# Two products of four column groups at the head of an MLP's up-projection

## The chip, the cores and the metric

One core of a Trainium2 chip runs the kernel. The metric is device microseconds of one execution, taken as the median of a few runs. The profile is of one more execution, with an instruction trace; its clock readings start at the first instruction.

## The reference

One layer of a hybrid decoder on x of 2048 positions by 1024 columns, float32. A mixer comes first (windowed attention beside a short convolution, with projections in and out), then

```python
x = x + y @ w_out[l]
hm = rms_norm(x, mlp_norm_g[l])
x = x + jnp.square(jax.nn.relu(hm @ w_up[l])) @ w_down[l]
```

with `w_up` 1024 x 4096 and `w_down` 4096 x 1024. The change is in the product `hm @ w_up`.

## The kernel before, in words

Every product of two float32 matrices is made of three passes of TensorE: an operand is split into a high part (a cast on ScalarE) and the rest (a subtraction on DVE), and high x high, high x low and low x high are summed in PSUM.

The up-projection works by Strassen's scheme in Winograd's form: seven products of blocks in place of eight, with sums of blocks before and behind them. The positions are two blocks of 1024 (`tb` 0 and 1), each 2 x 2 blocks of 512 x 512; the 4096 columns of `w_up` are 16 groups (`NCG`) of 256. A group n counts through both blocks, so n is 0 to 31, and a step of the loop is one product (n, p), p from 1 to 7: `NB` = 4 slices of 128 rows by three passes, 12 matmuls of 128x512 (L1118 to L1127). Products 1 and 2 add up in one PSUM bank, so do 5 and 3, and 7 and 4; banks tagged "at" (4) serve 1, 2, 5 and 3, those tagged "mm" (3) the others (L1115 to L1117).

The x operands of a block are seven matrices of 1 MiB, one a product p, that were written to DRAM (`xop_dram`) and are loaded in two halves of 512 KiB by `load_op` (L800), cast (L806) and subtracted (L807). They stay in the 14 `op` buffers for all 16 groups. The operands of block 0 are written by the last part of the mixer; those of block 1 are made during block 0 by the generator `prepare_rest` (L931), which takes one of its pauses at every step: it reads rows of `x1_dram` (L940), norms them (L943 to L946), transposes (L959), subtracts on GpSimd and stores (L977). What is left of it when the operands of block 1 are asked for is run at once (L1041).

The weights of a group are four pieces of 256 KiB (`Weights.pieces`, L838: for p = 1, 2, 7, 4), loaded at L849 in rows of 512 bytes. `sums` (L854) makes two more pieces on DVE (for 5 and 6) and changes that of 7 on GpSimd; `last` (L864) makes that of 3 on GpSimd. There are 18 buffers "w" for pieces. `split_up` (L869) casts and subtracts one product's piece (L872, L873).

`up_out` (L876) empties the PSUM bank behind a product: product 1 is copied to `u2` (L896), 2 gives a first result `f11` (relu and square on ScalarE, L899 and L888), which goes to DRAM (L882), 6, 5, 7, 3 and 4 add to it on DVE (L885), and behind 3 and 4 GpSimd forms four sums and differences (L814) that go to DRAM as well. Each kind of these tiles has one to three buffers (`UP_BUFS`, L60), and "st" has five, used by `prepare_rest`.

The order of the steps is the list `seq` (L992 to L1009). Each pass of the loop asks for the x operands of the step five ahead (`ready_x`, L1113) and for the weights of the step three ahead (`ready`, L1114), and then issues the 12 matmuls. Loads of x, of weights and of rows are all issued on the SP queue; a scheduler of the language may issue an instruction ahead of one that the code names first when its engine is free. The writes of the last chunk's rows to `x1_dram` come from GpSimd's queue (L634).

Of the kernel before, what the change touches and what calls it, by code (L numbers as in the profile page):

```python
# [52 lines left out]
NCG = DFF // (2 * P)  # L53
NTB = S // (2 * BW)

FIRST = (1, 6, 2)
LEAD, LEAD_DOWN = 3, 2
NOP = 14
DOWN_BUFS = {"u": 4, "x1": 5}
# [26 lines left out]
def hymba_layer(  # L86
# [44 lines left out]
    def bank(tag, name):  # L131
        return psum.tile([P, 512], F32, tag=tag, name=name, bufs=BANKS[tag])
# [29 lines left out]
    def rsqrt(dst, ms):  # L162

        nc.gpsimd.tensor_scalar(ms, ms, EPS, None, op0=ALU.add)
        nc.gpsimd.tensor_tensor(dst, ms, mhalf[:, : ms.shape[1]], op=ALU.pow)
# [647 lines left out]
    def tt(dst, a, b, op=ALU.subtract):  # L813
        nc.gpsimd.tensor_tensor(dst, a, b, op=op)  # L814


    def piece(tag, name):
        return pool.tile([P, BW], F32, tag=tag, name=name, bufs=UP_BUFS[tag])

    def pieces(blk):  # L820
        return blk.rearrange("p (k c) -> p k c", k=NB)
# [54 lines left out]
    def up_out(n, p, ps, v):  # L876

        tb, n = divmod(n, NCG)
        nm = f"{tb}_{n}"

        def put(i, b, eng):
            eng.dma_start(fop_dram[tb][ORDER_DOWN.index(i)][n // 2][:, n % 2], b)  # L882

        def add(dst, b):
            nc.vector.tensor_tensor(dst, ps, b, op=ALU.add)  # L885

        def square(b):
            nc.scalar.activation(b, b, AF.Square)  # L888

        def relu2(b):  # L890
            nc.scalar.activation(b, b, AF.Relu)  # L891
            square(b)

        if p == 1:
            v["u2"] = piece("u2", f"u2_{nm}")
            nc.scalar.copy(v["u2"], ps)  # L896
        elif p == 2:
            v["11"] = piece("f11", f"f11_{nm}")
            nc.scalar.activation(v["11"], ps, AF.Relu)  # L899
            square(v["11"])  # L900
            put(1, v["11"], nc.scalar)
        elif p == 6:
            add(v["u2"], v["u2"])
        elif p == 5:
            v["u4"] = piece("u4", f"u4_{nm}")
            add(v["u4"], v["u2"])
        elif p == 7:
            add(v["u4"], v["u4"])
            relu2(v["u4"])
            put(4, v["u4"], nc.scalar)  # L910
        elif p == 3:
            v["12"] = piece("f12", f"f12_{nm}")
            add(v["12"], v["u2"])
            relu2(v["12"])
            s1 = piece("s1", f"s1_{nm}")
            tt(s1, v["12"], v["u4"], ALU.add)
            put(5, s1, nc.gpsimd)
            v["s2"] = piece("s2", f"s2_{nm}")
            tt(v["s2"], s1, v["11"])
            put(6, v["s2"], nc.gpsimd)  # L920
            tt(v["12"], v["11"], v["12"])
            put(7, v["12"], nc.gpsimd)
        else:
            add(v["u2"], v["u2"])
            relu2(v["u2"])
            put(2, v["u2"], nc.scalar)
            s4 = piece("s4", f"s4_{nm}")
            tt(s4, v["u2"], v["s2"])
            put(3, s4, nc.gpsimd)

    def prepare_rest():  # L931

        xs = {}

        def fetch(t):
            for i in range(2):
                nm = f"m{2 + i}_{t}"
                r = 2 * BW + i * BW + t * P
                xt = pool.tile([P, D], F32, tag="xt", name=f"xt_{nm}", bufs=2)
                nc.sync.dma_start(xt, x1_dram[r : r + P, :])  # L940
                junk = piece("st", f"junk_{nm}").bitcast(BF16)[:, :D]
                ss = small.tile([P, 1], F32, tag="ss", name=f"ss_{nm}", bufs=2)
                nc.scalar.activation(junk, xt, AF.Square, scale=D**-0.5, accum_out=ss)  # L943
                rs = small.tile([P, 1], F32, tag="rs", name=f"rs_{nm}", bufs=2)
                rsqrt(rs, ss)
                nc.vector.tensor_scalar(xt, xt, rs, None, op0=ALU.mult)  # L946
                xs[i] = xt

        fetch(0)
        for _ in range(7):  # L950
            yield
        for t in range(NT):
            b = {}
            for i in range(2):
                for k in range(2):
                    nm = f"m{2 + i}_{t}_{k}"
                    pt = bank("tr", f"pt_{nm}")
                    for j in range(NB):
                        nc.tensor.transpose(  # L959
                            pt[:, j * P : (j + 1) * P], xs[i][:, (NB * k + j) * P : (NB * k + j + 1) * P], ident  # L960
                        )
                    b[k, i] = piece("st", f"st_{nm}")
                    nc.vector.tensor_tensor(
                        pieces(b[k, i]),
                        pieces(pt),
                        g_cols[:, NB * k : NB * (k + 1), None].to_broadcast([P, NB, P]),
                        op=ALU.mult,
                    )
                    yield
                    yield  # L970
            if t + 1 < NT:
                fetch(t + 1)
            yield

            def put(i, blk, t=t):
                dst = xop_dram[1][ORDER.index(i)].rearrange("p (k c) -> p k c", k=NB)
                nc.sync.dma_start(dst[:, :, t * P : (t + 1) * P], pieces(blk))  # L977

            b11, b21, b12, b22 = b[0, 0], b[1, 0], b[0, 1], b[1, 1]
            put(1, b11)  # L980
            put(2, b21)
            put(3, b22)
            for _ in range(3):
                yield
            for i, dst, b0, b1 in ((5, b11, b12, b11), (7, b12, b22, b12), (6, b22, b22, b11), (4, b21, b21, b22)):
                tt(dst, b0, b1)
                put(i, dst)
                yield

    seq, nf = [], 0  # L992

    def firsts(n):

        nonlocal nf
        for n in range(nf, min(n + 1, NTB * NCG)):
            yield from ((n, p) for p in FIRST)
        nf = max(nf, n + 1)

    for n in range(NTB * NCG):
        if not n:
            seq += sorted(firsts(1), key=lambda x: (1, 2, 6).index(x[1]))
        elif n % NCG in (0, NCG - 2):
            seq += firsts(n + 1)
        between = iter(list(firsts(n + 1)))
        for p in (5, 7, 3, 4):
            seq.append((n, p))
            seq += [x for x in (next(between, None),) if x]  # L1009
# [1 line left out]
    for i, (n, p) in enumerate(seq):  # L1011
        uses.setdefault((n // NCG, p), []).append(i)
    wts, wops, xops, ps, vs = {}, {}, {}, {}, {}
    others = prepare_rest()

    def ready(i):

        if i >= len(seq):
            return
        n, p = seq[i]  # L1020
        if n < 2 and p < 3:
            wts[n].piece(p, 1, p)
        if p == 1 and n > 1 or p == 6 and n == 1:
            for m in range(n, n + (3 if n > 1 else 2)):
                if m < NTB * NCG and m not in wts:
                    wts[m] = Weights(m)
        if p == 6 or p == 1 and n > 1:
            for m in range(n, n + (2 if p == 1 else 1)):
                if m < NTB * NCG and 5 not in wts[m].w:
                    wts[m].sums()  # L1030
        if p == 3:
            wts[n].last()
        wops[i] = split_up(wts[n].w[p], f"{n}_{p}")
# [64 lines left out]
    fill = ops.tile([P, 24], F32, tag="fill", name="fill")  # L1098
    nc.gpsimd.memset(fill, 0.0)

    for n in range(2):
        wts[n] = Weights(n, later=False)
    for i in range(LEAD):
        ready_x(i)
        ready(i)
    for i in range(LEAD, LEAD + 2):
        ready_x(i)
    for i, (n, p) in enumerate(seq):
        tb = n // NCG
        if i == len(seq) - NB:  # L1110
            for j in range(LEAD_DOWN):
                ready_down(j)
        ready_x(i + LEAD + 2)  # L1113
        ready(i + LEAD)  # L1114
        if p not in GOES_ON:  # L1115
            ps[n, AFTER.get(p)] = bank("at" if p in (1, 5) else "mm", f"u{n}_{p}")
        pt = ps[n, p if p in GOES_ON else AFTER.get(p)]  # L1117
        for k in range(NB):  # L1118
            for j, (a, b) in enumerate(((0, 0), (0, 1), (1, 0))):
                nc.tensor.matmul(  # L1120
                    pt,
                    wops[i][:, a, k, :],
                    xops[tb, p][k // 2][:, b, k % 2, :],
                    start=p not in GOES_ON and k + j == 0,
                    stop=k + j == NB + 1,
                    skip_group_check=True,
                )  # L1127
        up_out(n, p, pt, vs.setdefault(n, {}))

        if n > 1:  # L1130
            next(others, None)
    up_ctx.close()
    pool_tags.add("raw")
# [116 lines left out]
```

## Time and profile before

| what | value |
|---|---|
| runs | 2025.42, 2028.33, 2021.88 us; median 2025.42 |
| profiled execution | 2028.57 us |
| its span, first to last instruction | 2026.8 us |
| TensorE busy | 1958.5 us, 97% |
| DVE, ScalarE, GpSimd busy | 1309.6, 919.2, 607.2 us |
| mean granted TensorE clock | 0.983 |
| up-projection (L1120) | 752.2 to about 1401.6 us |

The profiled execution lasts 1.8 us longer than its span, and is 3.15 us above the median of the runs. An engine's busy time counts no DMA issue. Idle time of an engine is put down to the engine or transfer whose signal came last.

### The profile page before, as it was taken

To read this page: it belongs to the slowest core of one execution; us is meant where nothing else is said; L and a number is where in the kernel's file an instruction comes from. 1 tells how busy PE (TensorE), PEld (TensorE's weight loads), DVE (VectorE), ACT (ScalarE), POOL (GpSimd) and SP (SyncE) were. 2 spreads that over 40 slices of the span, in tenths; PEclk is the share of its full clock that TensorE was granted. 3 is DMA by queue.
4 is the path that set the end of the run, shared out by engine and by line. 5 is a ranking of instruction groups with operands and counts; after the bars stand their busy time and mean duration, and the time that the engine had idled before them with its cause. 6 is when DMAs were issued, how large, how long until landed. Compare 5 with 4: busy or idle time off the path is not lost.

```text
span 2026.8 us, 25559 instructions
## 1 busy us (share of the span) xinstructions
PE 1958.5 (97%) x9356; PEld 1632.9 (81%) x9356; DVE 1309.6 (65%) x1772; ACT 919.2 (45%) x1718; POOL 607.2 (30%) x647
## 2 busy tenths in 40 slices
PE   8999999999999987999998999999999999999989
PEld 7879887987988766888886888888788888888877
DVE  4787778678688878777868666665633434545551
ACT  5555455445555645555456455454432232231230
POOL 2231223313122324676654545544000000007000
PEclk9989999999999898999999999999999999999999
DMA  7214523352442477566757444435974447865551
GB/s 240 84 62 107 183 65 101 86 166 70 128 167 84 118 241 254 188 213 197 240 166 250 146 155 156 146 114 197 401 240 142 145 147 243 300 204 186 199 183 45
DMA packets 234190, 342.56 MB, mean 169 GB/s; under 512 B 17232, under 2 KB 148304, under 8 KB 234064
## 3 DMA queue, kind: packets, MB, share of 16 engines
q1 hardware_dynamic: 207120, 271.70, 41.9%
q0 software_dynamic: 13120, 44.05, 6.1%
q10 hardware_dynamic: 13824, 25.17, 3.3%
q8 instruction: 74, 1.21, 0.3%
q14 instruction: 52, 0.43, 0.1%
HBM read 242.31 MB, written 98.57 MB: 168 GB/s over the span
## 4 chain that ended last, share of the span: by engine, by line
PE 81%; DVE 6%; DMA 4%; POOL 3%; ACT 3%; issue 3%; SPq 0%; DVEq 0%; ACTq 0%; POOLq 0%
PE d L1212 29%; PE u L1120 26%; PE pout L212 2%; PE pout L214 2%; PE pout L213 2%; PE pz L213 2%; PE pz L212 2%; PE pz L214 2%; DMA op_x<-xop 2%; PE px_c L212 1%; PE px_c L213 1%; PE px_c L214 1%; PE pc_c L213 1%; PE pc_c L214 1%; PE pc_c L212 1%
## 5 line engine op out<-in xcount | busy, mean ns | idle before, releaser
L1120 PE MATMUL u<-op_x,wop 128*128 128x512 f32 x2688 | 624.7, 393 | 23.2 <-ACT u L896 10.0
L1212 PE MATMUL d<-op_w,op_f 128*128 128x512 f32 x2688 | 612.5, 390 | 8.5 <-DVE d L1166 6.9
L1120 PEld LDWEIGHTS u<-op_x,wop 128*128 128x128 f32 x2688 | 506.5, 189 | 134.9 <-ACT u L896 11.6
L1212 PEld LDWEIGHTS d<-op_w,op_f 128*128 128x128 f32 x2688 | 506.0, 188 | 114.8 <-issue 7.3
L807 DVE TENSOR_TENSOR op_f<-op_f 128x1024 fp32r<-128x1024 f32 x112 | 144.3, 1292 | 251.5 <-ACT op_f L806 251.4
L806 ACT CAST op_f<-op_f 128x1024 fp32r<-128x1024 f32 x112 | 117.5, 1051 | 329.3 <-DMA op_f<-fop 323.4
L873 DVE TENSOR_TENSOR wop<-wu,wop 128x512 fp32r<-128x512 f32 x160 | 190.1, 1192 | 68.2 <-ACT wop L872 68.1
L872 ACT CAST wop<-wu 128x512 fp32r<-128x512 f32 x160 | 98.7, 619 | 103.9 <-PE u L1120 92.5
L885 DVE TENSOR_TENSOR u<-u,u 128x512 f32<-128x512 f32 x128 | 87.5, 684 | 56.7 <-PE u L1120 56.4
L1075 POOL DMA_DIRECT2D wds<-raw x16 | 8.5, 534 | 333.4 <-DVE raw L1073 333.4
L807 DVE TENSOR_TENSOR op_w<-raw,op_w 128x1024 fp32r<-128x1024 f32 x56 | 73.1, 1305 | 34.0 <-ACT op_w L806 34.0
L806 ACT CAST op_w<-raw 128x1024 fp32r<-128x1024 f32 x56 | 58.9, 1052 | 64.8 <-PE d L1212 37.5
L814 POOL TENSOR_TENSOR wu<-wu,wu 128x512 f32<-128x512 f32 x32 | 42.9, 1342 | 136.6 <-DVE wu_s L859 136.6
L213 PE MATMUL pz<-w_qkv,h_h 128*128 128x256 f32 x288 | 82.3, 286 | 0.0
L212 PE MATMUL pz<-w_qkv,h_h 128*128 128x256 f32 x288 | 82.1, 285 | 0.0
L214 PE MATMUL pz<-w_qkv,h_h 128*128 128x256 f32 x288 | 81.6, 284 | 0.0
L477 POOL TENSOR_SCALAR_AFFINE_SELECT pp_b<-pp_b 128x512 fp32r<-128x512 f32 x60 | 48.3, 817 | 78.8 <-PE po_b L506 38.4
L891 ACT ACTIVATE u<-u 128x512 f32<-128x512 f32 x64 | 40.4, 632 | 65.6 <-DVE u L885 63.1
L873 DVE TENSOR_TENSOR wop<-wu_s,wop 128x512 fp32r<-128x512 f32 x64 | 65.9, 1029 | 3.1 <-ACT wop L872 3.1
L568 POOL COPY halo<-u_c 128x2 f32<-128x2 f32 x16 | 6.2, 386 | 200.2 <-DVE u_c L567 188.9
L872 ACT CAST wop<-wu_s 128x512 fp32r<-128x512 f32 x64 | 39.8, 622 | 57.4 <-PE u L1120 44.9
L814 POOL TENSOR_TENSOR s<-f,u 128x512 f32<-128x512 f32 x32 | 46.5, 1453 | 60.7 <-ACT f L888 60.7
(225 smaller groups left out, 3649.0 us busy)
## 6 DMA issues: line engine op xcount, KB each, us to landing
op_f<-fop SPq DMA_DIRECT2D x112, 512.0 KB, 4.2
raw<-in_w_down_dram SPq DMA_DIRECT2D x72, 512.0 KB, 4.2
wu<-in_w_up_dram SPq DMA_DIRECT2D x128, 256.0 KB, 3.5
fop<-s POOLq DMA_DIRECT2D x96, 256.0 KB, 2.5
fop<-u ACTq DMA_DIRECT2D x64, 256.0 KB, 3.1
op_x<-xop SPq DMA_DIRECT2D x28, 512.0 KB, 7.4
raw_qkv<-in_w_in_dram SPq DMA_DIRECT2D x11, 1024.0 KB, 5.4
x<-in_x_dram SPq DMA_DIRECT2D x20, 512.0 KB, 6.9
```

The costliest lines, as they stand in the source:

```text
L212: nc.tensor.matmul(ps, st(0), mv(0), start=first, stop=False)
L213: nc.tensor.matmul(ps, st(0), mv(1), start=False, stop=False)
L214: nc.tensor.matmul(ps, st(1), mv(0), start=False, stop=last)
L477: nc.gpsimd.affine_select(part, full, pattern=[[0, GQ], [1, P]], compare_op=ALU.is_ge, fill=0.0, base=0, channel_multiplier=-1,)
L806: nc.scalar.copy(op[:, 0], raw)
L807: nc.vector.tensor_tensor(op[:, 1], raw, op[:, 0].bitcast(F32), op=ALU.subtract)
L814: nc.gpsimd.tensor_tensor(dst, a, b, op=op)
L872: nc.scalar.copy(hi, blk)
L873: nc.vector.tensor_tensor(lo, blk, hi.bitcast(F32), op=ALU.subtract)
L885: nc.vector.tensor_tensor(dst, ps, b, op=ALU.add)
L1120: nc.tensor.matmul(pt, wops[i][:, a, k, :], xops[tb, p][k // 2][:, b, k % 2, :], start=p not in GOES_ON and k + j == 0, stop=k + j == NB + ...
L1212: nc.tensor.matmul(ps[tb][j], fs[tb][:, a, k, j * P : (j + 1) * P], w[:, b, k, :], start=first and p not in GOES_ON and k + n == 0, stop=l ...
```

## The change

The list of steps opens with products 1 and 2 of four groups (`START`) where it opened with products 1, 2 and 6 of two. Product 6 of groups 1 to 3 follows among the products 5, 7, 3, 4 of the group before. From group 4 on the list is as it was. For the first four groups a product's own piece is loaded alone (p = 1, 2); the other two pieces of groups 0 and 1 are loaded at (2,2) and (3,2), and those of 2 and 3 at (0,6) and (1,6). `prepare_rest` takes its first step at (3,5) and not at (2,1). `u2` of group 3 and `f11` of groups 2 and 3 lie in "st" buffers.

```diff
+START = 4
...
-            v["u2"] = piece("u2", f"u2_{nm}")
+            v["u2"] = piece("st" if tb == 0 and n == START - 1 else "u2", f"u2_{nm}")
...
-            v["11"] = piece("f11", f"f11_{nm}")
+            v["11"] = piece("st" if tb == 0 and START - 2 <= n < START else "f11", f"f11_{nm}")
...
-    seq, nf = [], 0
+    seq, nf = [], START
...
     for n in range(NTB * NCG):
         if not n:
-            seq += sorted(firsts(1), key=lambda x: (1, 2, 6).index(x[1]))
-        elif n % NCG in (0, NCG - 2):
+            seq += [(m, p) for p in (1, 2) for m in range(START)] + [(0, 6)]
+        elif n >= START and n % NCG in (0, NCG - 2):
             seq += firsts(n + 1)
-        between = iter(list(firsts(n + 1)))
+        between = iter([(n + 1, 6)] if n + 1 < START else list(firsts(n + 1)))
...
-    others = prepare_rest()
+    others, begin = prepare_rest(), seq.index((START - 1, 5))
...
-        if n < 2 and p < 3:
-            wts[n].piece(p, 1, p)
-        if p == 1 and n > 1 or p == 6 and n == 1:
-            for m in range(n, n + (3 if n > 1 else 2)):
+        if n < START:
+            if p < 3:
+                wts[n].piece(p, 1, p)
+
+            if p == 2 and n >= START - 2:
+                wts[n + 2 - START].pieces()
+            if p == 6:
+                wts[n].sums()
+                if n + 2 < START:
+                    wts[n + 2].pieces()
+                else:
+                    wts[n + 2] = Weights(n + 2)
+        elif p == 1:
+            for m in range(n, n + 3):
                 if m < NTB * NCG and m not in wts:
                     wts[m] = Weights(m)
-        if p == 6 or p == 1 and n > 1:
-            for m in range(n, n + (2 if p == 1 else 1)):
+            for m in range(n, n + 2):
                 if m < NTB * NCG and 5 not in wts[m].w:
                     wts[m].sums()
...
-    for n in range(2):
+    for n in range(START):
         wts[n] = Weights(n, later=False)
...
-        if n > 1:
+        if i >= begin:
             next(others, None)
```

## Rows read from the trace of the kernel before

**Rows 1.** The page, granted TensorE clock in 40 slices of 50.67 us, in tenths

```profile
PEclk9989999999999898999999999999999999999999
```

**Rows 2.** Four stretches: length, busy us of each engine (instructions), clock, DMA share, GB/s

```profile
752.00:762.00 10.00, 6.62 (x25) 4.64 (x26) 6.41 (x7) 4.10 (x7) 0.99 (x8) 1.00 1.04 407
762.00:772.00 10.00, 6.26 (x25) 4.25 (x24) 7.77 (x8) 9.14 (x13) 1.62 (x1) 1.00 1.07 373
772.00:782.00 10.00, 5.09 (x12) 3.17 (x11) 7.15 (x7) 1.89 (x3) 3.36 (x3) 0.60 1.07 346
782.00:792.00 10.00, 9.65 (x31) 7.48 (x32) 9.67 (x12) 5.95 (x9) 2.47 (x2) 0.72 0.87 243
```

**Rows 3.** TensorE's waits, 752 to 792: total us, times, longest us

```profile
PE u L1120 <- ACT wop L872: 7.0, 3, 3.0
PE u L1120 <- DVE wop L873: 3.5, 2, 2.5
```

**Rows 4.** ScalarE in order of time: start, us, line, names [idle before <-what ended it]

```profile
757.41 1.05 ACT L806 CAST op_x<-op_x 128x1024 fp32r<-128x1024 f32 x1 [1.64 <-DMA op_x<-xop]
760.52 0.62 ACT L872 CAST wop<-wu 128x512 fp32r<-128x512 f32 x1 [2.06 <-DMA wu<-in_w_up_dram]
```

**Rows 5.** DMA issues, 736 to 800 us: count, KB each, median us to landing

```profile
op_x<-xop SPq DMA_DIRECT2D x14, 512.0 KB, 8.8
...
xop<-xm SPq DMA_DIRECT2D x5, 256.0 KB, 3.1
xt_m<-x_dram SPq DMA_DIRECT2D x2, 512.0 KB, 4.5
```

**Rows 6.** TensorE in order of time, first and last of 34 matmuls

```profile
743.11 0.40 PE L214 MATMUL pout<-w_wo,at_b 128*128 128x512 f32 x1
...
750.61 0.39 PE L214 MATMUL pout<-w_wo,at_b 128*128 128x512 f32 x1
```

**Rows 7.** TensorE in order of time, 751 to 800

```profile
752.17 0.50 PE L1120 MATMUL u<-op_x,wop 128*128 128x512 f32 x1 [1.17 <-ACT wop L872]
...
754.71 5.07 PE L1120 MATMUL u<-op_x,wop 128*128 128x512 f32 x21 [1.01 <-DVE wop L873]
...
771.72 0.73 PE L1120 MATMUL u<-op_x,wop 128*128 128x512 f32 x2 [3.03 <-ACT wop L872]
774.96 4.63 PE L1120 MATMUL u<-op_x,wop 128*128 128x512 f32 x10 [2.50 <-DVE wop L873]
782.35 17.81 PE L1120 MATMUL u<-op_x,wop 128*128 128x512 f32 x66 [2.76 <-ACT wop L872]
```

**Rows 8.** ScalarE in order of time, the copy behind product (2,1)

```profile
804.28 0.59 ACT L896 COPY u<-u 128x512 f32<-128x512 f32 x1
```

**Rows 9.** DVE in order of time, GpSimd idle beside it

```profile
758.50 1.23 DVE L807 TENSOR_TENSOR op_x<-op_x 128x1024 fp32r<-128x1024 f32 x1 [1.46 <-ACT op_x L806]
761.17 0.69 DVE L873 TENSOR_TENSOR wop<-wu,wop 128x512 fp32r<-128x512 f32 x1 [1.45 <-ACT wop L872]
```

**Rows 10.** Issues of the SP queue in order of time, 742 to 790

```profile
760.52 3.77 SPq L805 DMA_DIRECT2D op_x<-xop  x3
765.28 8.57 SPq L849 DMA_DIRECT2D wu<-in_w_up_dram  x6
...
776.63 11.65 SPq L849 DMA_DIRECT2D wu<-in_w_up_dram  x8
788.33 0.97 SPq L940 DMA_DIRECT2D xt_m<-x_dram  x2
```

**Rows 11.** Groups of instructions, 788 to 860: busy us, mean ns | idle before

```profile
L873 DVE TENSOR_TENSOR wop<-wu,wop 128x512 fp32r<-128x512 f32 x18 | 23.3, 1300 | 3.8 <-ACT wop L872 3.7
...
L885 DVE TENSOR_TENSOR u<-u,u 128x512 f32<-128x512 f32 x15 | 10.2, 682 | 4.8 <-PE u L1120 4.8
...
L814 POOL TENSOR_TENSOR s<-s,f 128x512 f32<-128x512 f32 x3 | 3.9, 1304 | 0.1
```

**Rows 12.** TensorE's waits, 1040 to 1120: total us, times, longest us

```profile
PE u L1120 <- ACT u L896: 7.6, 1, 7.6
```

## The prediction, made before the changed kernel ran

> **What bounds the kernel now.** I read the busy shares by slice first. TensorE is the engine that sets the time, and its granted clock is near full but in three slices; the one inside the MLP begins at 760 us [rows 1]. So I cut the first 40 us of the MLP into four stretches: TensorE is busy for only 27.6 of 40 us, the clock falls to 0.60 and 0.72, and the DMA engines are full (share 1.04 to 1.07) until 782 us, with DVE next behind at 31.00 of 40 [rows 2]. The list of TensorE's waits there names casts and subtractions of weight pieces first [rows 3]; those engines waited for transfers in their turn, as ScalarE's own rows show: the cast of a half of x at 757.41 and that of a weight piece at 760.52 each start when a transfer lands [rows 4]. An x load took 8.8 us from issue to landing [rows 5]. So the start of the MLP is bound by transfers: 7 MiB of x operands and the weights go through one full queue, and TensorE's order asks for a new 1 MiB operand after every two products, or after one.
>
> How much is lost there: matmuls of 512 columns follow each other by 7.50 us / 33 = 0.227 us at the full clock [rows 6], so a product of 12 matmuls takes 2.73 us, and twelve products 32.7 us. In the trace the first begins at 752.17 [rows 7] and the twelfth in the order, (2,1), ends at about 804.2, when ScalarE copies it out [rows 8]: 52.0 us. The loss is 19.3 us, of which 12.4 are idle (40 less the four busy times [rows 2]). A clock of 0.60 and 0.72 over 20 us is 13.6 us at the lower of the two levels, 1.2 of 2.4 GHz [rows 2]; it starts behind the two gaps before 771.72 and 774.96 [rows 7], TensorE works in some 10 of them at half its rate, and so loses about 5. The rest are the ends of products. From 782.35 on TensorE runs without a gap that matters [rows 7]. Nothing over this 19.3 can be won.
>
> **The order of products.** Twelve products open the MLP now as (0,1) (1,1) (0,2) (1,2) (0,6) (1,6) (0,5) (0,7) (0,3) (0,4) (1,5) (2,1); after, as (0..3,1) (0..3,2) (0,6) (0,5) (1,6) (0,7). The number of matmuls is the same. Two operands now carry eight products, 21.8 us of work, in which the other five MiB can land. I follow the queue step by step.
> Until 760.52 the queue has delivered x1, x2 and three weight pieces [rows 4]. The new order has the same bytes ahead of that moment, only with the third piece before x2, so x2's second half lands at about 760.5 and not 757.4. Products (0,1), (1,1), (2,1) need x1 and one piece each: TensorE goes on where the first two now stop (754.71 + 5.07 = 759.8, of which 0.2 are the last one's end [rows 7]) and reaches 762.3. Product (3,1) has its piece behind x2: ScalarE casts x2's half (1.05) and the piece (0.62) [rows 4], DVE subtracts for the half (1.22) and the piece (0.68) [rows 9], so it is whole at 760.5 + 1.05 + 1.22 + 0.68 = 763.5. Two matmuls need no subtraction, so about 0.8 us are idle, and the product ends at 765.8.
> From 760.5 the queue moves 360 GB/s (mean of 373 and 346 [rows 2]). In the order of the new code, in MB after that point: three pieces 0.79, x6 1.84, a piece and two for group 0 2.62, x5 3.67, the piece of (3,2) 3.93, four pieces 4.98, x7 6.03, x3 7.08, two pieces 7.60, x4 8.65, and three results of 0.26 MB written meanwhile, 9.4 in all. The piece of (3,2) lands at 771.4 and is split by 773.3; TensorE wants it at 765.8 + 3 x 2.73 = 774.0. (0,6) is wanted at 776.7, with its pieces there since 767.8. (0,5) is wanted at 779.5; its cast stands behind those of x7, which lands at 777.3, so it is split at 777.3 + 1.05 + 1.22 + 0.68 = 780.2: 0.3 idle. (1,6) stands behind x3 in the same way (780.2, split at 783.1) and is wanted at 782.5: 0.3. (0,7) stands behind x4 (786.6, split at 789.6) and is wanted at 785.5: 3.6 idle if the engines keep the program's order, none if the splits are issued ahead. The twelfth product ends at about 791.8, against 804.2: **12.4 us won**; 15 to 16 with the splits ahead of x4. The engines do not always keep the order: the issue queue now has three x halves ahead of the six pieces of groups 1 and 2, and by the code it would be two [rows 10]. I take the strict order.
>
> **Weight loads.** Each product's own piece is loaded alone, and the other two of a group follow at products 2 and 6; by the time x4 is in, 16 pieces have gone and not 20. That is 1.05 MB less in the full queue, 2.9 us, and is in the sum above. The pieces of groups 4 to 6 are loaded together at (4,1), 12 of them with the first needed 3 steps or 8.2 us later; now 8 come at (2,1) into the full queue, and TensorE doesn't stop behind them [rows 7, 10]. Nothing.
>
> **The second block's preparation** starts at step 24 of the order instead of 11. Its DMA reads of rows at 788.33 [rows 10], its norms on ScalarE, GpSimd and DVE, its transposes and its seven stores per tile move later, none is added; the SP queue has weight loads alone ahead of them then. It has 71 pauses, one a step: it ends at step 95, before the change at 85. The operands are first asked for at step 104. Nine steps, 24.6 us, are left as cover; without it the cost is that of the slow case below.
>
> **Buffers.** Three results of groups 2 and 3 use the five "st" buffers, free until step 24, and are gone by step 30; no instruction is added. Four open accumulators take all four "at" banks; (0,5) wants the first one again at step 9, four steps or 11 us after (0,2) ended. Nothing.
>
> **Groups 0 to 2 closer together.** Their products 5, 7, 3, 4 and a 6 come five steps apart, 13.65 us, and not six or seven. Per group DVE has five splits and two sums (7 x 0.68) and five additions from PSUM (0.68 [rows 11]), 8.2 us; GpSimd six subtractions or additions of 1.3 [rows 11], 7.8. Each fits in 13.65, so I take 0. The other end: now, with GpSimd at work, a split takes 1.30 and not 0.68 [rows 9, 11], while the addition that reads PSUM stays at 0.68. If nothing on the two engines overlaps, a group needs 16.0 us, 2.35 too many, for three groups 7.0. The Trainium skill's "SBUF — State Buffer" (section "SBUF: two separate sides") says that DVE instructions with two SBUF inputs and GpSimd instructions lock a shared pair of ports, one blocking the other whole. The trace agrees, and by that rule the closer groups speak against the change; the lock alone would take 7 x 0.68 + 7.8 = 12.6 us of 13.65, no stop.
>
> **The sum.** The profiled execution is 2028.57 (span 2026.8 and 1.8 around it): 2028.57 - 12.4 = 2016.2. The median of the runs is 3.15 below it, so **2013.0** is the forecast. 0.3% (6.1 us) is about what a measurement of this kernel tells from no change.
>
> **Rivals.**
> A, as forecast, with 9 to 18 us won: 2007 to 2016. For it: idle time, full queue and order of use stand together in one stretch.
> B, DVE and GpSimd become the bound: at 31.00 of 40 us now [rows 2], DVE has no room for work that comes sooner, and the three groups give back 7.0: 12.4 - 7.0 = 5.4 won, 2020.0. Against it: between 788 and 860 the same mix ran beside a TensorE that never waited.
> C, the half clock stays, because the idle time of (3,1) or before (0,7) still brings it: a stretch like the present one costs about 5 us again: 7.4 won, 2018.
> D, nothing comes of it: the instruction order that is built is not the program's, as [rows 10] shows for one load, so x2 or the fourth piece waits in the queue and TensorE's idle time only moves to (3,1) and (0,7). Two to five won, about 2022.
> E, slower: at the border of the two blocks TensorE already waits 7.6 us once, behind a copy in ScalarE's queue [rows 12]. If the preparation, ten steps later than now, is not done by step 104, what is left of it runs ahead of the x loads. A tile that is left takes its read (4.5 [rows 5]), four subtractions on GpSimd (5.2 [rows 11]) and a store (3.1 [rows 5]), 12.8 us, and the load behind it 8.8; five steps (13.65) hide a part. One tile costs 8 us, two 20.8: 2025.4 - 12.4 + 20.8 = 2034. It decides when 9 of the 71 steps slip, and makes the kernel slower from some 25; by the count none does.
>
> **Chances.** A 0.57, B 0.13, C 0.12, D 0.12, E 0.06. A and C are faster by over 0.3%, and half of B: 0.75. The other half of B and D lie within: 0.19. Slower: 0.06. The range runs from all 19.3 won (2006) to the far side of D (2022); it leaves out E, and some of D.
>
> **What will show it.** Right: TensorE's idle time between 752 and 792 falls from 12.4 to under 6 us, with no clock below 0.9 there; (3,1) starts within 1.5 us of (2,1)'s end; the twelfth product ends near 792; DVE is at 35 us or more of those 40; the DMA share stays full until about 787. Wrong: a half clock after 760, a stop between 795 and 835 whose releaser is DVE or GpSimd (B), or a wait near 1069 that was 1.0 and is 10 or more (E).

## The result, and the profile after

The changed kernel takes 2012.9 us (median of 6 runs, 2010.07 to 2014.92), the one before 2024.12 beside it (6 runs). The ratio is 0.9944, with a 95% interval from 0.9931 to 0.9957: 11.3 us won, 8.7 to 14.0. The forecast was 2013.0.

The profiled execution lasts 2014.13 us, its span 2012.1. It is 14.4 us under that of before, which is more than the change gave: the mixer, whose instructions are the same and in the same order on every engine, ended 3.6 us sooner (747.4 against 751.0 us). The last section comes back to that. Times in the up-projection are therefore compared from the mixer's end; the stretches below are those of [rows 2] by the clock, and so lie 3.6 us later behind the mixer than before.

Four stretches after, for [rows 2], and the one behind them (length; busy us of PE, PEld, DVE, ACT, POOL with instructions; clock; DMA share; GB/s):

```profile
752.00:762.00 10.00, 10.00 (x46) 8.27 (x45) 6.15 (x7) 7.17 (x10) 0.33 (x5) 1.00 1.09 362
762.00:772.00 10.00, 9.34 (x42) 7.41 (x41) 7.20 (x8) 6.56 (x12) 2.63 (x2) 1.00 1.10 354
772.00:782.00 10.00, 6.78 (x27) 5.21 (x26) 9.85 (x9) 7.98 (x13) 5.80 (x4) 0.93 1.00 313
782.00:792.00 10.00, 9.72 (x39) 7.62 (x38) 10.00 (x14) 6.48 (x11) 6.64 (x6) 0.90 0.71 247
792.00:802.00 10.00, 10.00 (x46) 8.29 (x45) 10.00 (x9) 5.50 (x10) 7.91 (x8) 1.00 0.46 146
```

The DMA engines are as busy as before until 782 us, though they move 362, 354 and 313 GB/s in place of 407, 373 and 346. TensorE is busy for 35.8 of the 40 us up to 792 and not 27.6. DVE is busy for 29.85 of the 30 us from 772 on, so that it is now the next thing that can hold TensorE up. TensorE in order of time, for [rows 7]:

```profile
749.38 0.74 PE L1131 MATMUL u<-op_x,wop 128*128 128x512 f32 x2 [1.27 <-DVE op_x L809]
751.12 19.11 PE L1131 MATMUL u<-op_x,wop 128*128 128x512 f32 x83 [1.00 <-DVE wop L875]
770.89 5.75 PE L1131 MATMUL u<-op_x,wop 128*128 128x512 f32 x24 [0.66 <-DVE wop L875]
779.85 10.07 PE L1131 MATMUL u<-op_x,wop 128*128 128x512 f32 x36 [3.22 <-DVE wop L875]
```

One long run of seven products, a short wait before the third matmul of (3,2), then one wait of 3.2 us before the third matmul of (0,5), and behind it a stretch of lower clock of 3.4 us in place of 13.6. The twelfth product ends at 789.47, 42.07 us after the mixer; before it was 804.24 - 751.00 = 53.24. So 11.2 us are won there. By the 25th product, where the order is that of before again, 8.6 of them are left. TensorE's waits of 752 to 792, for [rows 3], are one row:

```profile
PE u L1131 <- DVE wop L875: 4.2, 3, 3.2
```

### The profile page after: what moved, and what is told of

Same layout as the page of the kernel before. It is cut to its first block, busy times and chain, and to the rows that moved or that the text cites. A ratio compares the mean times of both kernels' runs of the same rounds, so it can differ in the third digit from the quotient of the medians.

```text
span 2012.1 us, 25577 instructions
## 1 busy us (share of the span) xinstructions
PE 1950.2 (97%) x9356; PEld 1628.0 (81%) x9356; DVE 1312.1 (65%) x1772; ACT 919.5 (46%) x1718; POOL 611.3 (30%) x647
## 5 line engine op out<-in xcount | busy, mean ns | idle before, releaser
L875 DVE TENSOR_TENSOR wop<-wu_s,wop 128x512 fp32r<-128x512 f32 x64 | 60.3, 943 | 3.9 <-ACT wop L874 3.9
L449 ACT ACTIVATE sc_b<-sc_b,ngm_b 128x128 f32<-128x128 f32 x128 | 49.6, 390 | 28.5 <-DVE ngm_b L446 28.4
```

Of the source, the lines that this page charges most:

```text
L449: nc.scalar.activation(sc[:, hd, :], sc[:, hd, :], AF.Exp, bias=ngm[:, hd : hd + 1], accum_out=den[:, hd : hd + 1])
L875: nc.vector.tensor_tensor(lo, blk, hi.bitcast(F32), op=ALU.subtract)
```

## The experiments

Each ran five rounds beside the kernel before. "Won" is the ratio times 2024 us. One execution is profiled; "up stage" is measured in that trace, from the end of the mixer's last matmul to the end of the last up-product, so that it holds none of the mixer's spread. It has a spread of its own: "preparation late" and "group 2's pieces later", whose times can't be told from those of the kernel before, are 2.7 and 2.8 us shorter than it in this column, most of it at the border of the two blocks, where TensorE waits 7.6 us in the trace of before [rows 12] and 5.2 and 5.3 in theirs. The changed kernel waits 5.4 there, so some 2 of its 9.3 us can't be put down to the change.

| kernel | ratio, 95% interval | won, us | up stage, us |
|---|---|---|---|
| before | 1 | 0 | 650.9 |
| changed | 0.9944 (0.9931 to 0.9957) | 11.3 | 641.6 |
| START = 2 | 0.9955 (0.9938 to 0.9973) | 9.1 | 643.9 |
| START = 3 | 0.9965 (0.9951 to 0.9980) | 7.1 | 646.7 |
| whole groups loaded | 0.9969 (0.9956 to 0.9982) | 6.3 | 646.7 |
| before, preparation late | 0.9999 (0.9986 to 1.0012) | 0.2 | 648.2 |
| before, (1,6) later | 0.9985 (0.9970 to 1.0000) | 3.0 | 648.5 |
| before, group 2's pieces later | 0.9993 (0.9983 to 1.0003) | 1.4 | 648.1 |
| changed, x asked for last | 0.9966 (0.9953 to 0.9979) | 6.9 | 643.9 |
| changed, subtractions on DVE | 0.9949 (0.9936 to 0.9961) | 10.3 | 641.8 |
| before, new load plan | 0.9981 (0.9969 to 0.9994) | 3.8 | 644.9 |
| START = 2, x four ahead | 0.9988 (0.9977 to 1.0000) | 2.4 | 647.6 |
| changed, two groups on DVE | 0.9960 (0.9944 to 0.9976) | 8.1 | 641.0 |
| the same, border changed | 0.9934 (0.9919 to 0.9950) | 13.4 | 637.6 |

**Two groups in place of four.**

```diff
-START = 4
+START = 2
```

> The changed kernel with START = 2: products 1 and 2 of two groups open the MLP, (0,6) follows and (1,6) comes one place later; pieces are still loaded alone and the second block's preparation starts at (1,5). Theory O (the order: eight products on two x operands, 21.8 us of TensorE work, cover the loads of the other five): four products cover 10.9 us, 10.9 fewer than with four groups, of which the loads need nearly all, so the kernel stands near the one before, 2019 to 2025 us, with 9 us or more idle on TensorE between the first product and the twelfth. Rival W (loading pieces alone, 16 and not 20 in the full queue, is what wins): all of the weight change is here, so 2011 to 2016 us.

Theory O's total falls here: 9.1 us won, where it gave up to 5 and rival W 8 to 13. Its sign for the first twelve products holds, though: in the trace the twelfth ends 47.9 us after the mixer, 5.3 sooner than before and 5.9 later than with four groups, with 9.8 us idle behind the first matmul (O: 9 or more). The rest of the 9.1 isn't found in this trace, which is of the slowest of the seven runs (2016.94 us, median 2012.83). The stop is elsewhere than expected. TensorE's products in order of time:

```profile
758.97 3.02 PE L1131 MATMUL u<-op_x,wop 128*128 128x512 f32 x12 [1.91 <-ACT u L898]
766.77 1.22 PE L1131 MATMUL u<-op_x,wop 128*128 128x512 f32 x2 [4.79 <-ACT wop L874]
769.46 30.79 PE L1131 MATMUL u<-op_x,wop 128*128 128x512 f32 x124 [1.46 <-DVE wop L875]
```

and ScalarE's instructions ahead of that wait:

```profile
760.83 1.05 ACT L808 CAST op_x<-op_x 128x1024 fp32r<-128x1024 f32 x1 [1.92 <-DMA op_x<-xop]
...
762.26 1.05 ACT L808 CAST op_x<-op_x 128x1024 fp32r<-128x1024 f32 x1
...
763.70 1.04 ACT L808 CAST op_x<-op_x 128x1024 fp32r<-128x1024 f32 x1
...
765.17 1.04 ACT L808 CAST op_x<-op_x 128x1024 fp32r<-128x1024 f32 x1
...
766.10 0.62 ACT L874 CAST wop<-wu 128x512 fp32r<-128x512 f32 x1
```

The wait of 4.8 and 1.5 us stands before (1,2), whose piece had landed at 758.7; its cast stands behind those of four halves of x6 and x5 that were still coming in. After it 124 matmuls run without a stop. So with two groups the queue of ScalarE is what is waited for, once, and the later waits of the kernel before, 3.0 and 2.5 us at (0,6) and 2.8 before (1,6) [rows 7], are gone.

**Three groups** (`START = 3`).

> The changed kernel with START = 3: six products on x1 and x2, 16.4 us. Theory O: between, 2014 to 2020 us, some 5 us more idle than with four groups in the first twelve products. Rival W: as the changed kernel, 2011 to 2015 us. If DVE and not the transfers is what the wait before (0,5) hangs on, three groups may lose little: 2013 to 2016 us with a wait of 4 to 6 us before the first product on x5.

2015.7 us and 7.1 won lie in O's range, but fewer than with two groups (the intervals overlap). The profiled execution shows how little that says: TensorE's idle time in the first 100 us is 8.5 us (changed kernel 9.0, START = 2 10.6, before 13.4), yet the lower clock was granted for 17.1 us there and cost 8.0, against 1.7 in the changed kernel; 6.8 of the 17.1 us began 2.6 us after the mixer's end, in the first product, which stands in the same place in both. In idle time three groups do as well as four.

**The pieces of a group loaded together.**

```diff
             if p < 3:
-                wts[n].piece(p, 1, p)
+                wts[n].pieces()
```

> The changed kernel, but all four pieces of groups 0 to 3 are loaded at their product 1, twelve pieces (3.1 MB) ahead of x2 and not three. Theory O with my sum of the queue: x2 lands 2.36 MB or 6.5 us later, about 762 us, so (0,2) or already (3,1), whose piece is behind it, waits 3 to 6 us; 2015 to 2020 us. Rival W: most of the gain goes, 2020 us or more. If the queue has slack: within 1.5 us of the changed kernel.

6.3 us won, 5.0 fewer than the changed kernel (the intervals touch at 0.9956 and 0.9957). The order of four groups is worth something without its load plan, which W denies; the plan carries the rest, which O's sum gave as 3 to 6 us of wait. They are there, 3.0 and 1.0 us where the products of x1 end:

```profile
761.12 1.78 PE L1131 MATMUL u<-op_x,wop 128*128 128x512 f32 x6 [3.01 <-ACT wop L874]
763.86 15.71 PE L1131 MATMUL u<-op_x,wop 128*128 128x512 f32 x68 [0.97 <-DVE wop L875]
```

**The preparation of the second block later, alone.**

```diff
-        if n > 1:
+        if i >= 24:
             next(others, None)
```

> The kernel before, with one part of the change alone: the second block's preparation starts at step 24 and not at (2,1), step 11. Theory O: no loss before 782 us is touched by it, so 2022 to 2026 us, no change. Rival P (the preparation's work on DVE at 795 us and its 1 MiB of reads at 788 are what held the start): 2013 to 2018 us.

No change. Rival P is out: moving that work away doesn't help the kernel before, since TensorE's waits are over when it begins.

**Only (1,6) moved.**

```diff
             seq += sorted(firsts(1), key=lambda x: (1, 2, 6).index(x[1]))
+            seq.remove((1, 6))
...
-        between = iter(list(firsts(n + 1)))
+        between = iter(list(firsts(n + 1)) if n else [(1, 6)])
```

> The kernel before with one move: (1,6) comes behind (0,5), as the changed kernel with two groups has it, all loads in the old way. In the run with START = 2 no wait stood before (1,6), where the kernel before waits 2.76 us, and the waits before the product on x6 and the lower clock behind them stayed. Theory S (the sum pieces of 6 come too late, and the products ahead of them decide): 2.5 to 4 us of idle time less in the first 100 us, 2019 to 2022 us. Rival W (fewer pieces in the queue): no change, 2022 to 2025 us.

3.0 us won, at the edge of what can be told (interval up to 1.0000). The waits in the trace:

```profile
761.50 5.75 PE L1121 MATMUL u<-op_x,wop 128*128 128x512 f32 x16 [2.14 <-ACT wop L872]
768.10 4.83 PE L1121 MATMUL u<-op_x,wop 128*128 128x512 f32 x20 [0.85 <-DVE wop L873]
775.68 24.60 PE L1121 MATMUL u<-op_x,wop 128*128 128x512 f32 x94 [2.76 <-ACT wop L872]
```

Counted by matmuls (12 a product), the 2.1 us stand before (1,2), whose piece is its own; (0,6) waits 0.9 us in place of 5.5; and (1,6), the product that was moved, still waits 2.8. Idle time fell by 4.8 us in the first 100, more than S gave, and the lower clock took 2.8 of that back. The moved product isn't where the gain lies.

**Only group 2's pieces asked for later.**

```diff
-        if p == 1 and n > 1 or p == 6 and n == 1:
-            for m in range(n, n + (3 if n > 1 else 2)):
+        if p == 1 and n > 1:
+            for m in range(n, n + 3):
```

> The kernel before with one load moved: group 2's four pieces (1.05 MB) are asked for at (2,1) and no longer at (1,6), where they stand in the queue ahead of the pieces of (1,6) itself and of x3 and x4. Theory W: (1,6)'s pieces land 2.9 us sooner, its wait of 2.76 us goes and the products on x5 to x4 follow sooner: 2018 to 2021 us. Theory S alone: the wait moves by less than 1 us, 2022 to 2025 us. A loss is possible at (2,1), whose piece then comes in the middle of a full queue: a wait there of 2 us or more would show it.

No change that can be told, 1.4 us. The wait before (1,6) went from 2.8 to 2.0 us and those at (0,6) from 3.0 and 2.5 to 3.0 and 2.0. One MB less in the queue is not what wins.

**x operands asked for last in a pass.**

```diff
-        ready_x(i + LEAD + 2)
         ready(i + LEAD)
...
         up_out(n, p, pt, vs.setdefault(n, {}))
+        ready_x(i + LEAD + 2)
```

> The changed kernel; each pass of the loop asks for the x operands after the step's weights, its matmuls and the emptying of its bank, and not before. The prediction's step: (0,5), (1,6), (0,7) wait because a split stands behind casts and subtractions of x on ScalarE and DVE. Theory Q (order in the engines' queues): the 3.2 us before (0,5) fall under 1 us, and the copy behind the x casts at the border of the blocks (5.4 us) shrinks too: 2007 to 2011 us. Rival T (transfers are what is late): the wait moves to the first product on x7 or x3, since x is asked for later; 2012 to 2016 us.

A miss for Q: 6.9 us won, fewer than the changed kernel's 11.3. The 3.2 us did break up, into 1.9, 1.3 and 1.1 before three products, all waiting for DVE's subtraction of a weight piece. The wait at the border stayed (5.7 us). Moving x in the queues shares the wait out; it doesn't take DVE's work away. It isn't what makes this kernel the slower one in the traces: its twelfth product ends 41.2 us after the mixer, 0.8 sooner than in the changed kernel. It is 0.8 us behind that kernel at the 25th product, and 3.6 behind it past a wait at 1056, 2.9 us for the cast of a weight piece with 3.4 us of lower clock behind it, where the changed kernel waits 1.7.

**The weight subtractions of groups 0 to 3 on DVE.**

```diff
-            self.nm = f"wu{n}"
+            self.nm, self.early = f"wu{n}", n < START
...
-            tt(w[7], w[1], w[7])
+            (nc.vector if self.early else nc.gpsimd).tensor_tensor(w[7], w[1], w[7], op=ALU.subtract)
...
-            tt(self.w[2], self.w[2], self.w[6])
+            (nc.vector if self.early else nc.gpsimd).tensor_tensor(
+                self.w[2], self.w[2], self.w[6], op=ALU.subtract
+            )
```

> The changed kernel; for groups 0 to 3 the two subtractions of weight pieces (for products 7 and 3) are done by DVE and not by GpSimd. Theory G (DVE is held up by GpSimd: the subtractions of x7 took 2.3 us and not 1.22 while GpSimd was at work, 2 x 1.1, the split of (0,6) 1.3, that of (3,2) 1.8 for 0.68): DVE gets 2 x 0.68 us more of work in the stretch and 4 us less of hold-ups, the wait before (0,5) falls from 3.2 to 1 us or less, 2009 to 2012 us. Rival: DVE is full without GpSimd, its added work delays the splits: 2013 to 2016 us.

The wait before (0,5) is gone (0.6 us is the largest behind the first product's and up to 800 us). Most of that is G's cause: the split of (0,5) ends 30.6 us after the mixer's end in place of 32.4. The rest is chance: in this execution a lower clock in the first two products brought TensorE to (0,5) 1.7 us later. In the border experiment below, with the two groups that matter here changed in the same way and no lower clock, the split is there at 29.7 us and 1.5 us of wait are left before (0,5). DVE in the changed kernel, ahead of that wait:

```profile
772.12 1.30 DVE L875 TENSOR_TENSOR wop<-wu_s,wop 128x512 fp32r<-128x512 f32 x1 [0.69 <-ACT wop L874]
...
774.66 4.54 DVE L809 TENSOR_TENSOR op_x<-op_x 128x1024 fp32r<-128x1024 f32 x2
779.12 1.28 DVE L875 TENSOR_TENSOR wop<-wu_s,wop 128x512 fp32r<-128x512 f32 x2
```

GpSimd beside it:

```profile
771.57 1.30 POOL L816 TENSOR_TENSOR wu<-wu,wu_s 128x512 f32<-128x512 f32 x1 [1.28 <-DVE wu_s L863]
774.09 1.81 POOL L816 TENSOR_TENSOR wu<-wu,wu 128x512 f32<-128x512 f32 x1 [1.23 <-DVE wu_s L861]
775.85 2.26 POOL L816 TENSOR_TENSOR wu<-wu,wu_s 128x512 f32<-128x512 f32 x1
```

and DVE with those subtractions its own:

```profile
774.89 0.68 DVE L877 TENSOR_TENSOR wop<-wu_s,wop 128x512 fp32r<-128x512 f32 x1
...
776.82 1.22 DVE L809 TENSOR_TENSOR op_x<-op_x 128x1024 fp32r<-128x1024 f32 x1
777.95 0.68 DVE L864 TENSOR_TENSOR wu<-wu,wu 128x512 f32<-128x512 f32 x1
778.55 1.22 DVE L809 TENSOR_TENSOR op_x<-op_x 128x1024 fp32r<-128x1024 f32 x1
```

Two halves of x take 2 x 1.22 and not 4.54 us, the split 0.68 and not 1.30, and the subtraction itself 0.68 where GpSimd took 1.8 to 2.3. Yet the time is not better than the changed kernel's (10.3 won against 11.3): behind 800 us, where GpSimd forms the groups' sums, DVE now carries two subtractions more per group, and TensorE waits longer for its additions:

```profile
PE u L1133 <- DVE u L889: 4.5, 3, 1.9
```

against 2.4 us in two waits in the changed kernel. That is the place where the prediction had put rival B.

**The load plan alone, in the old order of products.**

```diff
-        if n < 2 and p < 3:
-            wts[n].piece(p, 1, p)
...
+        if n < 2:
+            if p < 3:
+                wts[n].piece(p, 1, p)
+            if p == 2:
+                wts[n].pieces()
+            if p == 6:
+                wts[n].sums()
+                wts[n + 2] = Weights(n + 2)
...
```

> The kernel before in its own order of products, with the load plan that the changed kernel has for two groups: the other pieces of groups 0 and 1 are asked for at (0,2) and (1,2), ahead of x5, and the four pieces of groups 2 and 3 behind the sums of 0 and 1. The move of (1,6) alone gave 4.0 us and the deferral of group 2's pieces 1.4, and START = 2 gave 9 to 11. Theory E (pieces asked for in the order in which they are needed are the rest): 4 to 7 us won, 2017 to 2020 us, with the waits before (0,6), 3.0 and 2.5 us, under 3 in all. Rival (only order and plan together give it, since the split of (1,2) stands behind the casts of x6 and x5 either way): 2020 to 2024 us.

3.8 us won, a little under E's range (4 to 7) and outside the other's upper half; the interval (1.2 to 6.3) holds both. The up stage is 6.0 us shorter in the trace. The waits:

```profile
759.31 0.73 PE L1125 MATMUL u<-op_x,wop 128*128 128x512 f32 x2 [0.49 <-ACT wop L872]
762.03 5.35 PE L1125 MATMUL u<-op_x,wop 128*128 128x512 f32 x22 [1.98 <-DVE wop L873]
769.91 1.02 PE L1125 MATMUL u<-op_x,wop 128*128 128x512 f32 x3 [2.53 <-ACT wop L872]
```

(0,6) doesn't wait at all, so E's sign (under 3 us) holds. The 0.5 and 2.0 us stand at (1,2), where the rival had looked for a wait, and 2.5 before (1,6) are left.

**Two groups, x asked for four steps ahead and last** (against the kernel with `START = 2`).

```diff
-    for i in range(LEAD, LEAD + 2):
+    for i in range(LEAD, LEAD + 1):
...
-        ready_x(i + LEAD + 2)
         ready(i + LEAD)
...
         up_out(n, p, pt, vs.setdefault(n, {}))
+        ready_x(i + LEAD + 1)
```

> START = 2, and x operands are asked for four steps ahead, behind the step's weights and the emptying of its bank, not five steps ahead and first. In the run with START = 2, TensorE waited 4.8 and 1.5 us before (1,2), whose piece had landed at 758.7 and was cast at 766.1 behind four casts of x6 and x5 halves. Theory Q (queue order on ScalarE and DVE): that wait falls under 2 us, the lower clock behind it goes, 4 to 6 us less lost there; 2008 to 2012 us. Rival T (the loads of x6 and x5 are then late themselves): a wait of 4 us or more before (0,6) or (0,5), 2013 to 2017 us.

Where Q looked it is right: the 4.8 and 1.5 us before (1,2) are gone, no wait up to 780 us is over 1.2, and the lower clock didn't come there (3.4 us of it came at 800). The total is a miss, 2.4 us won: with the shorter lead TensorE waits 2.9 us at 797 and 3.0 at 1056, and the rest of the up stage, behind its first 100 us, is 3.7 us longer than with START = 2. A lead that suits the first ten products is not the one for the others; a lead that changes on the way wasn't tried.

**The subtractions of groups 0 and 1 alone on DVE** (the edit above with `n < 2`).

> The changed kernel with the two subtractions of weight pieces on DVE for groups 0 and 1 alone. With all four groups on DVE the wait before (0,5) went from 3.2 to none, and waits for DVE's additions between 800 and 826 us grew from 2.4 to 4.5. Theory G (hold-ups in the first 40 us, DVE's own load behind them): no wait before (0,5), the later ones back near 2.5, TensorE's idle time in the first 100 us 5 to 6.5 us against 9.0; 2008 to 2012 us. Rival (the waits behind 800 come from the groups' being five steps apart, whatever engine subtracts): still 4 us or more there, 2011 to 2014 us.

8.1 us won: not told apart from the changed kernel. TensorE's idle time in the first 100 us is 7.0 against 9.0 us, less than G wanted; as in the run before, a lower clock in the first two products helped at (0,5). 1.8 us stay before a product at 786, and 1.3 and 1.9 at 804 and 820. These last two make 3.2 us, between G (near 2.5) and the rival (4 or more). The run with two groups, whose products stand further apart there, has no such wait, which speaks for the rival's cause, the groups' being five steps apart; it isn't shown.

**And (17,2) behind (16,5).**

```diff
+        held = [seq.pop()] if n == NCG else []
-        between = iter([(n + 1, 6)] if n + 1 < START else list(firsts(n + 1)))
+        between = iter([(n + 1, 6)] if n + 1 < START else held + list(firsts(n + 1)))
```

> The changed kernel with the two subtractions of groups 0 and 1 on DVE, and at the border of the two blocks (17,2) behind (16,5) and not ahead of it. At the border every run so far waited 5.3 to 7.6 us before (17,2), for the copy of (17,1) in ScalarE's queue, and a lower clock of 6.8 us followed. Theory Q (a product whose inputs are there can stand in front of one whose bank is not emptied, as eight products do at the head of the change): the wait falls by the 2.7 us of (16,5), to 3 us or less, and the low clock behind it may go; 2006 to 2010 us. Rival (the x operand of (16,5) is no earlier than the copy): the wait stays 5 us, before (16,5); 2010 to 2013 us.

13.4 us won, 2010.99 us, the lowest of all, though its interval (0.9919 to 0.9950) takes in the changed kernel's ratio. The cause of the shorter wait shows. TensorE at the border without the edit,

```profile
1079.67 6.74 PE L1133 MATMUL u<-op_x,wop 128*128 128x512 f32 x29
1092.04 8.23 PE L1133 MATMUL u<-op_x,wop 128*128 128x512 f32 x26 [5.63 <-ACT u L900]
```

and with it:

```profile
1084.65 5.37 PE L1134 MATMUL u<-op_x,wop 128*128 128x512 f32 x23
1091.16 2.56 PE L1134 MATMUL u<-op_x,wop 128*128 128x512 f32 x10 [1.14 <-DVE wop L877]
1096.05 4.14 PE L1134 MATMUL u<-op_x,wop 128*128 128x512 f32 x10 [2.33 <-ACT u L900]
```

The wait for the copy falls from 5.6 to 2.3 us with the product in front of it, less 1.1 us that this product waits itself. (The expectation has 5.3 to 7.6 us for every run before; the range in these traces is 3.8, with whole groups loaded, to 7.6.) The up stage is 3.4 us shorter than without the edit, near the spread of that column.

## Why the prediction was right

**The size** was right: 12.4 us forecast in the first twelve products, 11.2 found in the trace, 11.3 in the total. Not all of the agreement is merit. The trace keeps 8.6 of the 11.2 us past the 25th product, and its up stage gains some 2 again at the border, where kernels without the change gain them too. That the median is within 0.1 us of 2013.0 is luck: the kernel before ran 1.3 us faster beside it than the 2025.42 from which the sum starts, and the change gave 1.1 less than 12.4. **The bound** was right: the queue stays full until 782 us, and TensorE works through it.

Of the signs named, idle time between 752 and 792 fell to 4.2 us (under 6 wanted), the clock of no stretch is under 0.90, and (3,1) follows (2,1) without a gap. DVE is busy for 33.2 us there and not 35, and the queue is full to 782 and not 787. Two signs of being wrong came in small: the half clock for 3.4 us, and stops at 806 and 821 whose releaser is DVE.

**Product (3,1)**, 0.8 us of wait forecast: none. x2's second half was cast at 755.94, 8.5 us after the mixer's end where the queue's sum gave 9.5, and the piece behind it at 756.89:

```profile
755.94 1.05 ACT L808 CAST op_x<-op_x 128x1024 fp32r<-128x1024 f32 x1 [0.87 <-DMA op_x<-xop]
756.89 0.62 ACT L874 CAST wop<-wu 128x512 fp32r<-128x512 f32 x1
```

**(3,2)**, none forecast: 0.7. Its split took 1.78 us beside GpSimd and not 0.68.

**(0,5)**, 0.3 us forecast: 3.2. The form of the step held, the split stood behind x7's, though the two sums of group 1's pieces (0.68 and 0.69 us) stood ahead of x7's as well; and the terms 1.22 and 0.68 did not hold. With GpSimd at work a half of x7 took 2.3, and the split of (0,6) ahead of it 1.3. The prediction had a split at 1.30 beside GpSimd in its rows, but used it for the groups behind 790 us only. The experiments with DVE's own subtractions bring this split 1.8 to 2.7 us sooner, and so show that these prices were most of the wait.

**(0,7)**, 3.6 us forecast: none. Its cast was issued at 778.84, ahead of those of x4 (782.41 and 783.88), so the loose end of that step ("none if the splits are issued ahead") was the right one, and the strict order that I took was not. The two errors, 2.9 us too few at (0,5) and 3.6 too many at (0,7), nearly cancel; the rest of the gap is 1.7 us that the lower clock cost behind the wait before (0,5).

**Groups closer together**, 0 forecast, up to 7.0 by the upper bound: 2.4 us of waits for DVE's additions in two places. Between the ends, near the lower, and the 2.6 us that are given back between the twelfth and the 25th product.

**What was wrong is the share of the parts.** The prediction gave the whole gain to eight products on two operands and held the loads of weights for 2.9 us of queue time inside that sum. With four products on them, two groups, 9.1 of the 11.3 us are there (5.5 to 12.5). The load plan alone gives 3.8, the move of (1,6) 3.0, one MB less in the queue 1.4 or nothing, the later preparation nothing; plan and move together come to 6.8, within the two-group kernel's interval. The traces say where. Asking for the pieces of the sums ahead of x5 takes away the wait at (0,6); plan and move together take away that before (1,6) too, which the move alone leaves at 2.8 us; and each time a part comes back before (1,2): 2.1 us with the move, 2.5 with the plan, 6.3 with both. What four groups add to two is 5.9 us at the twelfth product and 4.3 at the 25th in the two traces, as the prediction's reasoning has it, but 2.3 at the end of the up stage and 2.2 in the ratios, which is under what these runs resolve. So how the gain is shared between four groups and two is left open.

The rivals: B's mechanism is real, and sits earlier than B had it; C came in part, 3.4 us of lower clock that cost 1.7; D did not come; of E there is no trace: the wait ahead of the border is 1.7 us and not 10, and that for the copy is 5.4 us and not 7.6, as in kernels without the change.

## What to carry to other kernels

When a stage starts on a full queue, put the work that needs least in front, and ask for the pieces of a sum ahead of an operand that is used later than the sum. Take the price of an instruction from rows in which its neighbour on the other engine is at work, if it will be; here that changed 2.4 us into 4.5. And a product whose inputs are there can be put in front of one that waits for its bank: at the border that made 3.5 us of waits out of 5.6, in one trace of each.

## What the runs showed of the hardware

The same instructions in the same order took the mixer from 743.1 to 751.0 us in these profiles, with no difference in what TensorE waited for (32.6 to 34.3 us idle); the difference lies in how long the lower clock was granted. Before (the columns of the table of stretches above):

```profile
0.00:751.00 751.00, 718.40 (x3916) 612.94 (x3916) 569.32 (x1031) 398.30 (x980) 199.73 (x261) 0.97 0.40 123
```

and in the run with the preparation late:

```profile
0.00:743.00 743.00, 708.78 (x3916) 605.39 (x3916) 568.57 (x1031) 398.25 (x981) 198.97 (x261) 0.99 0.40 125
```

TensorE is busy for 9.6 us more in the one, at 0.97 of the clock and not 0.99, for the same 3916 matmul records. The 96 runs of the kernel before beside the experiments spread over 12.5 us (2016.86 to 2029.35), and their clock goes with their time: those at 0.983 or less took 2024.1 to 2029.4 us, those at 0.990 or more 2017.0 to 2021.8. That is as much as this change is worth: a stretch must be compared from its own start, and a gain of this size by its idle time and many runs, not by two profiles.

DVE and GpSimd hold each other up. In all fourteen traces of the up-projection, DVE took 0.67 to 0.70 us for a subtraction or sum of two 128x512 weight pieces while GpSimd had no operation of 128x512 at work, and 1.5 us on average, up to 4.3, when one overlapped. GpSimd took 1.28 to 1.31 us for such an operation while DVE was idle, and up to 2.28 beside it. The Trainium skill's "SBUF — State Buffer" (section "SBUF: two separate sides") describes it as one shared pair of ports that the later instruction waits for; the rows above agree, and the addition that reads PSUM stayed at 0.67 to 0.69 us beside GpSimd in every run.
